# Row-tiled state updates of the samples, and the inverse's second triangle by VectorE's block transposes

## The chip, the core and the metric

One core of a Trainium2 chip. TensorE (PE) multiplies, with its weight loads on a lane of their own (PEld); VectorE (DVE), ScalarE (ACT) and GpSimd (POOL) work on the vectors, SyncE (SP) issues most transfers. The metric is the device time of one launch in microseconds, median of three runs.

## The reference, cut to what matters

Two layers of a hybrid decoder. Each projects 320 tokens (256 of a prompt; 8 samples of 8 tokens) through `W_in`, runs three mixers beside each other (gated DeltaNet, GDN; differential attention; gated linear attention, GLA), projects through `W_out`, and ends in a SwiGLU block. The change touches two pieces. The first is the triangular solve of GDN, whose matrix is the identity plus a strictly lower triangle:

```
A = where(strict, kk * dmat * bh[..., :, None], 0);  M = I + A
sol = triangular_solve(M, [vbeta, kbd], lower=True, unit_diagonal=True)
```

The second is the state update of the samples, in GDN and in GLA, for each head and sample:

```
S_new = S * exp(glast) + einsum('bhck,bhcv->bhkv', kw, u)     # GDN, 128 x 128 a head
S_new = S * exp(blast) + einsum('bchd,bchv->bhdv', kw, vi)    # GLA, 64 x 128 a head
```

The 64 sample tokens lie in 64 rows (partitions), 8 rows a sample.

## The kernel before, in words

**Dense work.** The weights stream in 1,616 units of 128x512. ACT rounds a unit to `whi`, DVE takes the rest as `wlo` (`conv_hi`, `conv_lo`), and PE runs 12 matmuls of 128x320 a unit, in a fixed order. All else on PE (the mixers) is written by tasks (`gdn_prompt`, `gdn_sample`, `gla_prompt`, `gla_sample`, attention) and is put between the dense matmuls by a list scheduler, `Program.order`, which fixes the order of every engine ahead of the launch from its own table of costs. Nearly every instruction is recorded through one helper, so the profile has them all on line 673 and they are told apart by tile and shape. Small matmuls that follow each other and write different quarters of the partitions are kept together as one piece of work by `Program.add` and `_merge`. An fp32 matmul stands once in an order and as two passes in the trace.

**The inverse** (`inverse`, line 1530). It runs on the 32x32 blocks of the diagonal, with R = 128 rows for a prompt chunk (4 blocks, 3 heads, 5 levels) and R = 64 for the samples (2 blocks, 3 heads, 3 levels). A tile `tu` holds the inverse so far (`tu[:,0]`) and its transpose (`tu[:,1]`). Both are kept current by matmuls: first one group against `idb`, then at each level a group that gives `p_`, a copy by ACT, and two groups, one for each form. A group is 12 matmuls of 32x32 for the prompt, 6 for the samples. There are 8 prompt inverses and 4 of samples in the two layers.

**The samples' states.** `gdn_sample` (line 1780) and `gla_sample` (line 2360) hold the states of the 8 samples side by side in a tile `s0` of 128x1024. The update takes two steps `a`, one for each half of the samples: the values are spread over four blocks of 128 columns with the mask `ind8`, a matmul over all 64 rows gives 512 columns, and DVE adds them to half of `s0`. Both steps spread into the same tile, so the second spread waits for the first matmul. In GDN DVE spreads the first and POOL the second; in GLA each step has one spread on either. Then `s0` is written out and the next head's state loaded into it.

**The end of the mixers.** `gate` multiplies GDN's outputs `sv` by the gates, head by head, into `oA` (a rounded copy by ACT, the rest by DVE). The first `out` units of a layer read `oA`.

Of the kernel before, what the change touches and what calls it, by code (L numbers as in the profile page):

```python
# [18 lines left out]
ALU = mybir.AluOpType  # L19
# [274 lines left out]
def raw_ap(x):  # L294
    x = x.ap_ if isinstance(x, LazyAP) else x
    return x if isinstance(x, bass.AP) else x[:]
# [46 lines left out]
class Program:  # L343
# [36 lines left out]
    def add(self, e, name, fn, a, kw, lab, reads, writes):  # L380
        o = Op()
        i = o.i = len(self.ops)
        o.e, o.name, o.fn, o.a, o.kw, o.lab, o.hold = e, name, fn, a, kw, lab, self.hold
        o.func = str(a[2]).split(".")[-1] if name == "activation" else None
        if o.func not in SETS:
            o.func = None
        o.dense = e == "PE" and isinstance(lab, tuple) and lab[0] == "unit" and a[1].dtype == F32R
        out = kw.get("out", a[0] if a else None)
        if e == "PE" and out.shape[0] < 128 and self.ops:
            p = out.start_partition() // 32  # L390
            quads = set(range(p, p + (out.shape[0] + 31) // 32))
            g = self.ops[-1]
            if g.e == "PE" and g.lab == lab and len(g.quads) < 4 and not quads & set(g.quads):
                self._merge(g, o, reads, writes, quads)
                return g
        deps, raw, o.quads, psum = set(), set(), None, False
        for w, aps in ((False, reads), (True, writes)):
            for ap in aps:
                r = region(ap)
                if r is None:  # L400
                    continue
                key, p0, p1, spans = r
                if key.startswith("bank"):
                    psum, spans = True, [(0, 512)]
                    deps.update(self.pre.get(key, ()))
                    self.seen.setdefault(key, []).append(i)
                if w and e == "PE":
                    o.quads = range(p0 // 32, (p1 + 31) // 32)
                    for q in o.quads:
                        if (key, q) in self.chain:  # L410
                            deps.add(self.chain[(key, q)])
                        self.chain[(key, q)] = i
                self._touch(i, key, w, p0, p1, spans, deps, raw)
        if o.dense:
            if self.last_dense is not None:
                deps.add(self.last_dense)
            self.last_dense = i
        deps.discard(i)
        o.preds, o.succs, o.n, o.subs, o.raw, o.table = deps, [], 0, [(fn, a, kw)], raw, None
        self._cost(o, psum)  # L420
        self.ops.append(o)
        return o

    def _merge(self, g, o, reads, writes, quads):

# [295 lines left out]
def emit(nc, pool, psp, T, O, coff, ioff, n_pages):  # L721
# [30 lines left out]
    banks = [psp.tile([128, 512], F32, name=f"bank{i}") for i in range(8)]  # L752
# [32 lines left out]
    def cs(name, rows=slice(0, 128)):  # L785
        a, n = coff[name]
        return cst[rows, a:a + n]


    def mm(out, lhsT, rhs, start=True, stop=True):  # L790
        PE.matmul(out, lhsT, rhs, start=start, stop=stop, skip_group_check=True)
# [6 lines left out]
    def tt(eng, out, a, b, op):  # L798
        eng.tensor_tensor(out=out, in0=a, in1=b, op=op)
# [79 lines left out]
    def ap(h):  # L879
        return h[1][2]  # L880

    def bank(n=1):
        if clk.task.t > clk.t["PE"] + SLACK:
            yield
        while len(dense_free if wide[0] else mix_free) < n:
            yield WAIT
        bs = [(dense_free if wide[0] else mix_free).popleft() for _ in range(n)]
        for b_ in bs:
            prog.epoch(f"bank{b_}")
        return bs if n > 1 else bs[0]  # L890

    def fb(*bs):
        for b in bs:
            free_dense(b)
# [635 lines left out]
    def inverse(aq, k, R, get, keep):  # L1530

        nb = R // 32
        lv = (1, 2, 4, 8, 16) if R == 128 else (1, 2, 4)
        nl = len(lv)
        Ad = yield from get(32 * k)
        ad = ap(Ad)[0:R].rearrange("p (h i) -> p h i", h=k)
        for b in range(nb):
            sl = slice(32 * b, 32 * b + 32)
            (G.tensor_copy if b % 2 else V.tensor_copy)(ad[sl], aq[sl, :, 1, sl])
        LT = yield from get(nl * 32 * k)  # L1540
        lt = ap(LT)[0:R].rearrange("p (s h i) -> p s h i", s=nl, h=k)
        msk = cs("ms", slice(0, R)).rearrange("p (s i) -> p s i", s=5)[:, 0:nl]
        for s in range(nl):
            tt(V, lt[:, s], ad, msk[:, s:s + 1, :].to_broadcast([R, k, 32]), ALU.mult)
        fr(Ad)
        yield
        TU = yield from keep(64 * k)
        tu = ap(TU)[0:R].rearrange("p (t h i) -> p t h i", t=2, h=k)
        idb = cs("idb", slice(0, R))[:, None, :].to_broadcast([R, k, 32])
        bb = yield from bank()  # L1550
        pv_ = banks[bb][0:R, 0:32 * k].rearrange("p (h i) -> p h i", h=k)
        for h in range(k):
            for b in range(nb):
                sl = slice(32 * b, 32 * b + 32)
                mm(pv_[sl, h], lt[sl, 0, h], cs("idb", sl))
        tt(G, tu[:, 1], idb, lt[:, 0], ALU.subtract)
        tt(V, tu[:, 0], idb, pv_, ALU.subtract)
        fb(bb)
        yield
        Ph = yield from get(32 * k)  # L1560
        p_ = ap(Ph)[0:R].rearrange("p (h i) -> p h i", h=k)
        for s in range(1, nl):
            bb = yield from bank()
            pv_ = banks[bb][0:R, 0:32 * k].rearrange("p (h i) -> p h i", h=k)
            for h in range(k):
                for b in range(nb):
                    sl = slice(32 * b, 32 * b + 32)
                    mm(pv_[sl, h], lt[sl, s, h], tu[sl, 0, h])
            A.copy(p_, pv_)
            fb(bb)  # L1570
            yield
            bb = yield from bank()
            pw = banks[bb][0:R, 0:64 * k].rearrange("p (t h i) -> p t h i", t=2, h=k)
            for h in range(k):
                for b in range(nb):
                    sl = slice(32 * b, 32 * b + 32)
                    mm(pw[sl, 0, h], tu[sl, 1, h], p_[sl, h])
                for b in range(nb):
                    sl = slice(32 * b, 32 * b + 32)
                    mm(pw[sl, 1, h], p_[sl, h], tu[sl, 1, h])  # L1580
            tt(V, tu, tu, pw, ALU.subtract)
            fb(bb)
            yield
        fr(LT, Ph)
        return TU
# [194 lines left out]
    def gdn_sample(l, hs):  # L1780
# [9 lines left out]
        TU = yield from inverse(aq, 3, 64, tmp, get)  # L1790
# [7 lines left out]
        for k in range(3):  # L1798
# [34 lines left out]
            stt(osm[:, k], kq[64:128], col["egc"][64:128, 2, h:h + 1], b[64:128, 0:128], ALU.mult, ALU.add)  # L1833
            fb(bb)
            A.activation(sv[:, 9:137], osm[:, k], AF.Square, accum_out=sv[:, k:k + 1])
            for a in range(2):
                wm = ap(E)[0:64].rearrange("p (b v) -> p b v", b=4)
                tt(G if a else V, wm, ws[:, None, :].to_broadcast([64, 4, 128]),
                   cs("ind8", slice(0, 64))[:, 4 * a:4 * a + 4].unsqueeze(2).to_broadcast([64, 4, 128]), ALU.mult)
                yield  # L1840
                bb = yield from bank()
                b = banks[bb]
                mm(b, ap(KW)[0:64], ap(E)[0:64])
                tt(V, ap(S0)[:, 512 * a:512 * a + 512], ap(S0)[:, 512 * a:512 * a + 512], b, ALU.add)
                fb(bb)
            SP.dma_start(O["gs"][l, h], s0)
        fr(WS)
        rms_factor(sv[:, 0:3], sv[:, 3:6], sv[:, 6:9], col["rq"][64:128, 2, h0:h0 + 3])
# [511 lines left out]
    def gla_sample(l, bc, eb):  # L2360
# [29 lines left out]
        for k in range(3):  # L2390
# [18 lines left out]
            tt(V, o[:, k], o[:, k], b2[:, 256:384], ALU.add)  # L2409
            fb(bb[1])  # L2410
            A.activation(st[:, 9:137], o[:, k], AF.Square, accum_out=st[:, k:k + 1])
            for a in range(2):
                for e in range(2):
                    tt(V if e == a else G, four_(w[0:64, 512 * e:512 * e + 512]), vt[:, e:e + 1, :].to_broadcast([64, 4, 128]),
                       cs("ind8", slice(0, 64))[:, 4 * a:4 * a + 4].unsqueeze(2).to_broadcast([64, 4, 128]), ALU.mult)
                bb = yield from bank()
                for e in range(2):
                    h = 2 * k + e
                    mm(banks[bb][64 * e:64 * e + 64, :], kw[:, h * 64:h * 64 + 64], w[0:64, 512 * e:512 * e + 512])
                tt(V, s0[:, 512 * a:512 * a + 512], s0[:, 512 * a:512 * a + 512], banks[bb], ALU.add)  # L2420
                fb(bb)
            SP.dma_start(O["ls"][l, k], s0)
            if k < 2:
                SP.dma_start(s0, T["sgla"][l, k + 1])
# [190 lines left out]
```

## Time and profile before

| | |
|---|---|
| median of 3 runs | 3334.94 us (3334.14 to 3335.1) |
| the profiled execution: its own time, its span | 3333.0 us, 3331.3 us |
| granted TensorE clock, mean | 0.994 |
| PE, PEld, DVE, ACT, POOL busy | 98%, 93%, 59%, 45%, 12% of the span |
| chain that ended last | PE 91%, DVE 3%, DMA 2% |

The mixers of the first layer lie between about 120 and 660 us, those of the second between 1780 and 2320; outside these PE runs dense units nearly alone. PE's busy share counts a matmul from its start to its modelled end, which overlaps its neighbours, so the distance from one start to the next is the better measure.

### The profile page before, as it was taken

To read this page: it belongs to the slowest core of one execution; us is meant where nothing else is said; L and a number is where in the kernel's file an instruction comes from. 1 tells how busy PE (TensorE), PEld (TensorE's weight loads), DVE (VectorE), ACT (ScalarE), POOL (GpSimd) and SP (SyncE) were. 2 spreads that over 40 slices of the span, in tenths; PEclk is the share of its full clock that TensorE was granted. 3 is DMA by queue.
4 is the path that set the end of the run, shared out by engine and by line. 5 is a ranking of instruction groups with operands and counts; after the bars stand their busy time and mean duration, and the time that the engine had idled before them with its cause. 6 is when DMAs were issued, how large, how long until landed. Compare 5 with 4: busy or idle time off the path is not lost.

```text
span 3331.3 us, 69934 instructions
## 1 busy us (share of the span) xinstructions
PE 3271.5 (98%) x26570; PEld 3088.4 (93%) x26570; DVE 1966.5 (59%) x3734; ACT 1491.0 (45%) x3069; POOL 389.1 (12%) x634
## 2 busy tenths in 40 slices
PE   9999999999999999999999999999999999999997
PEld 9987887899999999999999878878999999999997
DVE  5676547886445444544776764588854544454445
ACT  5444444456433443344574543444644334433444
POOL 0234323200000000000002343231000000000000
PEclk9999999999999999999999999999999999999998
DMA  7456654455555555555555577534555555555553
GB/s 227 136 185 213 221 176 122 132 150 156 151 150 149 151 150 149 149 151 150 151 154 142 175 226 225 162 121 148 147 151 149 151 150 150 151 149 149 150 151 114
DMA packets 264404, 527.86 MB, mean 158 GB/s; under 512 B 31362, under 2 KB 33026, under 8 KB 263938
## 3 DMA queue, kind: packets, MB, share of 16 engines
q1 hardware_dynamic: 243586, 456.26, 47.6%
q0 software_dynamic: 20480, 67.13, 6.3%
q8 instruction: 208, 3.41, 0.4%
q14 instruction: 130, 1.06, 0.1%
HBM read 506.25 MB, written 16.36 MB: 157 GB/s over the span
## 4 chain that ended last, share of the span: by engine, by line
PE 91%; DVE 3%; DMA 2%; issue 2%; ACT 1%; POOL 0%; POOLq 0%; SPq 0%; ACTq 0%; DVEq 0%
PE bank L673 91%; DVE gen L673 1%; DVE wlo L673 1%; DMA geng<-in_ck 1%; DMA gen<-in_sgdn 0%; DMA c<-in_sgdn 0%; DVE geng L673 0%; SPq L673 0%; POOLq L2012 0%; DMA out_gs<-gen 0%; POOL geng L673 0%; DMA out_gs<-c 0%; ACT geng L673 0%; DVE blkB L673 0%; DMA raw<-in_win 0%
## 5 line engine op out<-in xcount | busy, mean ns | idle before, releaser
L673 DVE TENSOR_TENSOR wlo<-raw,whi 128x512 fp32r<-128x512 f32 x1616 | 1126.9, 698 | 1110.8 <-PE bank L673 903.3
L673 ACT CAST whi<-raw 128x512 fp32r<-128x512 f32 x1616 | 1002.1, 621 | 1423.9 <-PE bank L673 1347.2
L673 PE MATMUL bank<-xh,wlo 128*128 128x320 f32 (+1 forms) x4544 | 1422.8, 313 | 0.0
L673 PE MATMUL bank<-xh,whi 128*128 128x320 f32 (+1 forms) x4544 | 1416.7, 312 | 4.7 <-ACT xh L673 4.7
L673 PE MATMUL bank<-xl,whi 128*128 128x320 f32 (+1 forms) x4544 | 1416.4, 312 | 0.1
L673 PEld LDWEIGHTS bank<-xh,whi 128*128 128x128 f32 x4544 | 858.2, 189 | 20.8 <-issue 13.4
L673 PEld LDWEIGHTS bank<-xh,wlo 128*128 128x128 f32 x4544 | 859.8, 189 | 8.8 <-issue 5.4
L673 PEld LDWEIGHTS bank<-xl,whi 128*128 128x128 f32 x4544 | 857.6, 189 | 8.8 <-issue 6.2
L673 PE MATMUL bank<-actA,whi 128*128 128x320 f32 x1152 | 255.5, 309 | 0.0
L673 PEld LDWEIGHTS bank<-actA,whi 128*128 128x128 f32 x1152 | 193.0, 188 | 0.4
L673 PE MATMUL bank<-actA,wlo 128*128 128x320 f32 x576 | 178.2, 309 | 0.0
L673 PE MATMUL bank<-actB,whi 128*128 128x320 f32 x768 | 170.5, 309 | 0.0
L673 PE MATMUL bank<-actCh,whi 128*128 128x320 f32 x448 | 138.4, 309 | 0.0
L673 PE MATMUL bank<-actCh,wlo 128*128 128x320 f32 x448 | 138.3, 309 | 0.0
L673 PE MATMUL bank<-actCl,whi 128*128 128x320 f32 x448 | 138.3, 309 | 0.0
L673 PEld LDWEIGHTS bank<-actB,whi 128*128 128x128 f32 x768 | 128.6, 188 | 0.0
L673 PE MATMUL bank<-actB,wlo 128*128 128x320 f32 x384 | 118.6, 309 | 0.0
L673 PE MATMUL bank<-geng,gen 128*32 128x256 f32 (+5 forms) x968 | 111.5, 471 | 6.5 <-DMA geng<-in_ck 4.8
L673 PEld LDWEIGHTS bank<-actA,wlo 128*128 128x128 f32 x576 | 108.3, 188 | 0.1
L673 POOL COPY gen<-g 128x24 f32<-128x24 f32 x18 | 5.8, 328 | 871.9 <-DMA g<-in_scv 870.4
L2014 POOL DMA_DIRECT2D geng<-in_ck x128 | 70.3, 550 | 242.6 <-DVE actA L673 130.9
L673 PEld LDWEIGHTS bank<-g 32*32 32x32 f32 (+2 forms) x2784 | 55.9, 111 | 41.0 <-issue 29.7
(294 smaller groups left out, 3434.7 us busy)
## 6 DMA issues: line engine op xcount, KB each, us to landing
raw<-in_wgu SPq DMA_DIRECT2D x704, 256.0 KB
raw<-in_win SPq DMA_DIRECT2D x434, 256.0 KB
raw<-in_wd SPq DMA_DIRECT2D x352, 256.0 KB
geng<-in_ck POOLq DMA_DIRECT2D x128, 256.0 KB, 3.7
geng<-in_cvp POOLq DMA_DIRECT2D x128, 256.0 KB, 3.8
raw<-in_wout SPq DMA_DIRECT2D x128, 256.0 KB
c<-in_sgdn SPq DMA_DIRECT2D x6, 512.0 KB
out_gs<-c SPq DMA_DIRECT2D x6, 512.0 KB
```

The lines of the kernel that those rows point to most:

```text
L673: fn(*[real(x) for x in a], **{k: real(v) for k, v in kw.items()})
L2014: G.eng.dma_start(out[:, k * 512:k * 512 + 512], src[l, ds(reg, 1)].rearrange(pat))
```

## The change

**Inverse.** The group against `idb` goes: `tu[:,1]` is now taken on DVE (before on POOL) and `tu[:,0]` is its transpose, block by block, by `V.transpose`. At each level only `tu[:,0]` is updated by matmuls; `tu[:,1]` is again DVE's transpose of it. By the orders of the two kernels 552 matmuls of 32x32 go (480 of the prompt, 72 of the samples) and 52 transposes come (40 of 128x96, 12 of 64x96); DVE's subtractions at the levels halve from 192 to 96 columns, and 12 small subtractions move from POOL to DVE.

**State updates.** The values are spread once, with the mask `m4`, which repeats every 32 rows. Rows 0 to 31 hold samples 0 to 3 and rows 32 to 63 samples 4 to 7, so two matmuls over 32 rows each give the two halves, into two banks that are taken together. `_beside` lets the planner keep such matmuls together. The number of matmuls stays (24 in GDN, 24 in GLA); 12 spreads in GDN fall away from POOL, and in GLA 6 each from DVE and POOL.

```diff
+        if e == "PE" and name == "matmul" and self.ops and self._beside(self.ops[-1], o):
+            self._merge(self.ops[-1], o, reads, writes, set(self._cells(a)[1]))
+            return self.ops[-1]
...
+    def _beside(self, g, o):
+
+        if g.e != "PE" or g.name != "matmul" or g.lab != o.lab or o.a[1].shape[0] > 32:
+            return False
+        rows, cols, b = self._cells(o.a)
+        for _, a, _ in g.subs:
+            if a[1].shape != o.a[1].shape:
+                return False
+            r_, c_, b_ = self._cells(a)
+            if set(c_) & set(cols) and (set(r_) & set(rows) or b_ == b):
+                return False
+            if set(r_) & set(rows) and b_ != b:
+                return False
+        return True
...
-        bb = yield from bank()
-        pv_ = banks[bb][0:R, 0:32 * k].rearrange("p (h i) -> p h i", h=k)
-        for h in range(k):
-            for b in range(nb):
-                sl = slice(32 * b, 32 * b + 32)
-                mm(pv_[sl, h], lt[sl, 0, h], cs("idb", sl))
-        tt(G, tu[:, 1], idb, lt[:, 0], ALU.subtract)
-        tt(V, tu[:, 0], idb, pv_, ALU.subtract)
-        fb(bb)
+        tf, tf_ = (ap(TU)[0:R, 32 * k * t:32 * k * t + 32 * k] for t in range(2))
+        tt(V, tu[:, 1], idb, lt[:, 0], ALU.subtract)
+        V.transpose(tf, tf_)
...
             for h in range(k):
                 for b in range(nb):
                     sl = slice(32 * b, 32 * b + 32)
-                    mm(pw[sl, 0, h], tu[sl, 1, h], p_[sl, h])
-                for b in range(nb):
-                    sl = slice(32 * b, 32 * b + 32)
-                    mm(pw[sl, 1, h], p_[sl, h], tu[sl, 1, h])
-            tt(V, tu, tu, pw, ALU.subtract)
+                    mm(pw[sl, h], tu[sl, 1, h], p_[sl, h])
+            tt(V, tu[:, 0], tu[:, 0], pw, ALU.subtract)
             fb(bb)
+            V.transpose(tf_, tf)
...
+            wm = ap(E)[0:64].rearrange("p (b v) -> p b v", b=4)
+            tt(V, wm, ws[:, None, :].to_broadcast([64, 4, 128]),
+               cs("m4", slice(0, 64)).unsqueeze(2).to_broadcast([64, 4, 128]), ALU.mult)
+            yield
+            bb = yield from bank(2)
             for a in range(2):
-                wm = ap(E)[0:64].rearrange("p (b v) -> p b v", b=4)
-                tt(G if a else V, wm, ws[:, None, :].to_broadcast([64, 4, 128]),
-                   cs("ind8", slice(0, 64))[:, 4 * a:4 * a + 4].unsqueeze(2).to_broadcast([64, 4, 128]), ALU.mult)
-                yield
-                bb = yield from bank()
-                b = banks[bb]
-                mm(b, ap(KW)[0:64], ap(E)[0:64])
-                tt(V, ap(S0)[:, 512 * a:512 * a + 512], ap(S0)[:, 512 * a:512 * a + 512], b, ALU.add)
-                fb(bb)
+                sl = slice(32 * a, 32 * a + 32)
+                mm(banks[bb[a]], ap(KW)[sl], ap(E)[sl])
+            for a in range(2):
+                s_ = ap(S0)[:, 512 * a:512 * a + 512]
+                tt(V, s_, s_, banks[bb[a]], ALU.add)
+            fb(*bb)
```

`gla_sample` changes in the same way: two spreads with `m4` ahead of one group of four matmuls (two heads, two halves).

**Three places in the order.** PE, first layer, a level of a prompt's inverse (tile `g`) among attention's small matmuls. Before, a level's two groups are 12 and 24 matmuls:

```order
L673 MATMUL bank_80<-xh,wlo 128x320
L673 MATMUL bank_85<-g_0_90 32x32 x12
L673 MATMUL bank_86<-geng,gen 32x512 x4
L673 MATMUL bank_84<-g_0_90 32x32 x24
L673 MATMUL bank_83<-geng,gen 128x128 x2
```

After, both are 12:

```order
L696 MATMUL bank_81<-xl,whi 128x320
L696 MATMUL bank_85<-g_0_90 32x32 x12
L696 MATMUL bank_84<-geng,gen 32x256 x4
L696 MATMUL bank_82<-blkB,gen 32x64 x4
L696 MATMUL bank_85<-g_0_90 32x32 x12
```

PE, first layer, the first state update of the second three GDN heads (state in tile `gen`). Before, the two halves stand 11 dense matmuls apart:

```order
L673 MATMUL bank_81<-xh,whi 128x320
L673 MATMUL bank_83<-gen 128x512
L673 MATMUL bank_81<-xl,whi 128x320
...
L673 MATMUL bank_81<-xh,wlo 128x320
L673 MATMUL bank_83<-gen 128x512
```

After, they stand side by side:

```order
L696 MATMUL bank_80<-xh,whi 128x320
L696 MATMUL bank_82<-gen 128x512
L696 MATMUL bank_86<-gen 128x512
L696 MATMUL bank_84<-gen 64x128
L696 MATMUL bank_80<-xl,whi 128x320
```

Over the whole program the dense work is interrupted 344 times, before 356 times.

DVE, first layer, the gate of GDN ahead of the first `out` unit (`blkB` holds the gates). Before, the weight conversions `wlo` stand between its parts:

```order
L673 TENSOR_TENSOR blkB<-blkB,sv 128x320 x3
L673 TENSOR_TENSOR wlo<-raw,whi 128x512
L673 TENSOR_TENSOR oA_6448<-blkB,oA_6448 128x320 x3
L673 TENSOR_TENSOR wlo<-raw,whi 128x512
L673 TENSOR_TENSOR oA_6448<-blkB,oA_6448 128x320
```

After, it runs in one piece:

```order
L696 SCALAR_TENSOR_TENSOR blkB<-gen,blkB 128x960 x2
L696 TENSOR_TENSOR blkB<-blkB,sv 128x320 x3
L696 TENSOR_TENSOR oA_6182<-blkB,oA_6182 128x320
L696 TENSOR_TENSOR blkB<-blkB,sv 128x320
L696 TENSOR_TENSOR oA_6182<-blkB,oA_6182 128x320 x5
L696 TENSOR_TENSOR wlo<-raw,whi 128x512 x2
```

On PE the transposes that bring the last three GDN heads of the samples into `sv` stood 85 dense matmuls ahead of the first one that reads `oA`; after the change 25.

## Rows read from the trace of the kernel before

**Rows 1.** The page, busy time of the engines: us, share, instructions.
```profile
PE 3271.5 (98%) x26570; PEld 3088.4 (93%) x26570; DVE 1966.5 (59%) x3734; ACT 1491.0 (45%) x3069; POOL 389.1 (12%) x634
```
**Rows 2.** Stretches: length, busy (x) of PE, PEld, DVE, ACT, POOL, PEclk, DMA share, GB/s.
```profile
440.00:660.00 220.00, 210.32 (x2229) 175.76 (x2228) 162.04 (x306) 98.63 (x225) 67.22 (x60) 0.97 0.43 129
1000.00:1050.00 50.00, 50.00 (x343) 50.00 (x342) 26.10 (x43) 17.57 (x29) 0.00 (x0) 1.00 0.53 152
```
**Rows 3.** Timeline of PE at 448: start, us, engine, line, instruction.
```profile
447.77 0.30 PE L673 MATMUL bank<-xl,whi 128*128 128x320 f32 x1
448.01 0.39 PE L673 MATMUL bank<-g 32*32 32x32 f32 x24
448.33 0.41 PE L673 MATMUL bank<-xh,wlo 128*128 128x320 f32 x1
```
**Rows 4.** Timeline of PE, the dense matmuls around another burst.
```profile
125.80 0.31 PE L673 MATMUL bank<-xl,whi 128*128 128x320 f32 x1
...
126.53 0.42 PE L673 MATMUL bank<-xh,wlo 128*128 128x320 f32 x1
```
**Rows 5.** Groups of PE in 125.7 to 126.9: what that burst holds.
```profile
L673 PE MATMUL bank<-cst,g 32*32 32x32 f32 x24 | 0.4, 192 | 0.0
L673 PE MATMUL bank<-cst,c 32*32 32x32 f32 x12 | 0.4, 194 | 0.0
```
**Rows 6.** Groups of PE by form, whole span: busy us, mean ns | idle before, releasers.
```profile
L673 PE MATMUL bank<-g 32*32 32x32 f32 x2544 | 41.6, 195 | 0.1
...
L673 PE MATMUL bank<-gen,sq 128*32 128x512 f32 x24 | 7.2, 622 | 6.3 <-DMA gen<-in_sgdn 6.3
```
**Rows 7.** Timeline of PE at 167: half a GDN state update alone.
```profile
167.15 0.30 PE L673 MATMUL bank<-xh,whi 128*128 128x320 f32 x1
167.39 1.12 PE L673 MATMUL bank<-c 64*128 64x512 f32 x2
168.44 0.41 PE L673 MATMUL bank<-xl,whi 128*128 128x320 f32 x1
168.69 0.31 PE L673 MATMUL bank<-xh,wlo 128*128 128x320 f32 x1
```
**Rows 8.** Timeline of PE: attention's scores, two row halves, then one.
```profile
347.52 0.70 PE L673 MATMUL bank<-blkB 64*128 64x256 f32 x4
348.15 0.41 PE L673 MATMUL bank<-xh,whi 128*128 128x320 f32 x1
...
355.65 0.70 PE L673 MATMUL bank<-blkB 64*128 64x256 f32 x2
356.27 0.41 PE L673 MATMUL bank<-xl,whi 128*128 128x320 f32 x1
```
**Rows 9.** Timeline of PE: half a GLA state update, two heads, and what follows.
```profile
599.05 1.08 PE L673 MATMUL bank<-geng,gen 64*64 64x512 f32 x4
600.06 0.88 PE L673 MATMUL bank<-geng 128*64 128x128 f32 x12
```
**Rows 10.** Groups of DVE by form, whole span.
```profile
L673 DVE TENSOR_TENSOR g<-g,bank 128x192 f32<-128x192 f32 x32 | 11.3, 352 | 37.3 <-PE bank L673 36.9
L673 DVE TENSOR_TENSOR g<-g,cst 128x96 f32<-128x96 f32 x40 | 8.9, 262 | 1.6 <-POOL g L673 1.6
L673 DVE COPY geng<-geng 32x192 f32<-32x192 f32 x10 | 8.2, 819 | 0.3
```
**Rows 11.** Timeline, the last state updates and the gate of the first layer.
```profile
565.38 1.09 PE L673 MATMUL bank<-gen 64*128 64x512 f32 x2 [1.65 <-ACT geng L673]
...
573.08 0.40 PE L673 MATMUL bank<-cst,gen 64*128 64x64 f32 x3
...
590.75 0.34 PE L673 MATMUL bank<-oA,whi 128*128 128x320 f32 x1
```
**Rows 12.** The same stretch on DVE.
```profile
579.88 4.03 DVE L673 TENSOR_TENSOR blkB<-blkB,sv 128x320 f32<-128x320 f32 x3
...
588.05 0.48 DVE L673 TENSOR_TENSOR oA<-blkB,oA 128x320 fp32r<-128x320 f32 x1
```

More of the change, by code (lines that the diff above doesn't have):

```diff
@@ L422, in add, with _cells @@
         return o
+    def _cells(self, a):
+        k, p = a[1].start_partition() // 32, a[0].start_partition() // 32
+        return (range(k, k + (a[1].shape[0] + 31) // 32), range(p, p + (a[0].shape[0] + 31) // 32), raw_ap(a[0]).name)
+    def _beside(self, g, o):
[11 more added lines that the diff above has]
+        return True
     def _merge(self, g, o, reads, writes, quads):
@@ L1572, in inverse @@
             bb = yield from bank()
-            pw = banks[bb][0:R, 0:64 * k].rearrange("p (t h i) -> p t h i", t=2, h=k)
+            pw = banks[bb][0:R, 0:32 * k].rearrange("p (h i) -> p h i", h=k)
             for h in range(k):
@@ L2411, in gla_sample @@
             A.activation(st[:, 9:137], o[:, k], AF.Square, accum_out=st[:, k:k + 1])
+            for e in range(2):
+                tt(G if e else V, four_(w[0:64, 512 * e:512 * e + 512]), vt[:, e:e + 1, :].to_broadcast([64, 4, 128]),
+                   cs("m4", slice(0, 64)).unsqueeze(2).to_broadcast([64, 4, 128]), ALU.mult)
+            bb = yield from bank(2)
             for a in range(2):
[L2413 to L2416, printed above, removed]
+                sl = slice(32 * a, 32 * a + 32)
                 for e in range(2):
                     h = 2 * k + e
-                    mm(banks[bb][64 * e:64 * e + 64, :], kw[:, h * 64:h * 64 + 64], w[0:64, 512 * e:512 * e + 512])
-                tt(V, s0[:, 512 * a:512 * a + 512], s0[:, 512 * a:512 * a + 512], banks[bb], ALU.add)
-                fb(bb)
+                    mm(banks[bb[a]][64 * e:64 * e + 64, :], kw[sl, h * 64:h * 64 + 64], w[sl, 512 * e:512 * e + 512])
+            for a in range(2):
+                tt(V, s0[:, 512 * a:512 * a + 512], s0[:, 512 * a:512 * a + 512], banks[bb[a]], ALU.add)
+            fb(*bb)
             SP.dma_start(O["ls"][l, k], s0)
```

## The prediction

> **What bounds the kernel now.** I read the page's busy times first. PE is busy for 98% of the span and no other engine for more than 59% [rows 1], so the question is whether that is work or an average that hides waits. [...] In the last part of the first layer's mixers, 440 to 660, PE is still busy for 210 of 220 us at a granted clock of 0.97, with DVE busy for 162 and POOL for 67 [rows 2]. [...] The reader should take from this that a microsecond removed from PE in the mixers is a microsecond off the span, as long as the chains of the mixers still end before the dense work that needs them.
>
> What a mixers' burst costs is read from the timeline, by starts. Around a burst of 24 small passes the dense starts lie 0.56 us apart (447.77 to 448.33) [rows 3]; around one of 36 passes they lie 0.73 apart [rows 4, 5]. Twelve passes more cost 0.17, so 14 ns a pass. Over the whole span 2,544 such passes keep PE busy for 41.6 us, 16.4 ns each [rows 6], which counts the tail of each burst too. Half of a GDN state update takes two passes, and from its start to the next dense one it is 1.05 us (167.39 to 168.44); standing alone it pushes the second dense matmul behind it to 168.69, 1.54 after the one ahead of it. Two dense steps are 0.29 and the passes 1.05, so the interruption itself costs 0.20 [rows 7].
>
> **The change, part by part.** *Inverse, PE.* 552 matmuls go, 1,104 passes. At 15 ns, between the 14 and the 16.4, that is 16.6 us. The upper bound is 1,104 times 16.4, 18.1 us. For the lower one I drop the 144 passes of the samples, whose groups are so small that a burst of them may cost no less when it is halved: 960 times 14 ns is 13.4 us.
>
> *State updates, PE.* If two matmuls over different 32 rows run beside each other, each pair takes what one takes now. Twelve second halves in GDN at 1.05 us are 12.6 us. In GLA one half with its two heads takes 1.01 us from its start to the next group (599.05 to 600.06) [rows 9]; six of them are 6.1 us. Does the chip run two row halves side by side? Attention shows it by chance. Once its two score matmuls, which read the upper and the lower 64 rows and write different banks, stand together: four passes from 347.52 to the next dense start at 348.15, 0.63 us. Alone, two passes take from 355.65 to 356.27, 0.62 us [rows 8]. The second pair is free. Thirty-two rows in place of 64 are not shown here, so the bounds are nothing and the whole 18.7; I take the whole, since the nearest row shows no loss at all.
>
> *Interruptions.* Twelve fewer, at 0.20, are 2.4 us. If all twelve bursts fell away only in part, this is nothing.
>
> PE's sum is 16.6 + 12.6 + 6.1 + 2.4 = 37.7 us.
>
> *DVE.* Fifty-two transposes are new, and no row shows one. The nearest row, 96 columns from memory to memory, takes 0.262 us; the dearest plain copy of similar size takes 0.819 [rows 10]. I take 0.26, 13.6 us in all, and keep 0.82 (42.6 us) for the range. Against it the 36 subtractions of a level shrink from 192 columns (0.352 us) towards 96 (about 0.26), 3.3 us less, and 12 small ones come from POOL, 3.1 us more. So DVE gains some 13 us over two layers. I cost that at nothing: in the busiest stretch DVE has 58 of 220 us free [rows 2], and a transpose is not what comes next in its chain. The next level's first group reads `tu[:,0]`, which the subtraction has just written; only the second group reads the transpose, after PE's first group and ACT's copy. Behind a transpose in DVE's queue stand the weight conversions, and PE waits for these if DVE falls behind by the lead of its buffers. Without cover the price is the full 13.6. [...]
>
> *Chains.* A head's update had two steps in a row, which read and wrote one spread tile. In the second three heads of GDN they now become one, so `s0` is written out, and the next head's load behind it on SP's queue issues, that much earlier. PE also eats the dense units faster, though. What is late next is the gate. Before, the samples' last outputs were transposed at 573.08 and the first `out` matmul started at 590.75, 17.7 us later [rows 11]; DVE's last part of `oA` ended at 588.53 [rows 12]. After the change only 24 dense matmuls stand between, and the whole gate is one piece on DVE. Behind the transposes (0.40) come three products (4.03 together [rows 12]), one more and six subtractions at 0.48 each: about 7.8 us. PE reaches the sixth block of `oA` after 24 and 15 dense matmuls, 5.7 us. It waits some 2 us a layer, 4 in all. The lower bound is nothing, if the products find their inputs early. The upper one is the chain as long as it was: 588.53 less 573.08 is 15.5, less 5.7, so 9.8 a layer and 19.6 in all.
>
> **The sum.** 3331.3 - 37.7 + 4 = 3297.6 us of span. The profiled execution's own time was 1.7 above its span, and the runs' median is 1.9 above that execution: 3301 us.
>
> **The rivals.** *The row tiles take turns.* Then the 18.7 us of the state updates stay, PE saves 37.7 - 18.7 - 4 = 15 and the time is 3320. Attention's pair speaks against it [rows 8], though its tiles have 64 rows; for it speaks only that no row shows 32. [...]
>
> *The gate comes too late.* PE's savings ahead of `oA` are about 31 us in two layers (all but GLA's), so PE arrives some 15 us earlier a layer. If the sample chain moves less than that, because its loads and DVE's queue set it and not PE, the wait is nearer its upper bound, 15 to 20 us in all: 3313 to 3317. For it speaks how short the lead has become in the order; against it that the chain loses a whole step a head.
>
> *Waits of before close as well.* The trace has PE waiting 1.65 us for ACT ahead of one state update [rows 11] and 6.3 us for the second heads' states [rows 6]. If the shorter chains take these, a wait of the first kind in either layer and most of the second kind, 8 us, and the gate costs nothing, the time is 3289.
>
> *DVE becomes the bound.* This ends on the other side. If a transpose takes 0.82 us and none of it is covered, the conversions behind it make PE wait 42.6 us and the time is 3344. It decides from 33.7 / 52 = 0.65 us uncovered a transpose. The 58 us free in the busiest stretch speak against it.
>
> *The change does not do what it says:* PE's work shrinks and the time stays, since the stream of weights sets the pace of the mixers. The DMA share is 0.43 in 440 to 660 and 0.53 in the dense stretch [rows 2], so there is room, and I give this little: 3335.
>
> **How the numbers follow.** Forecast as summed, within 3294 to 3309: 0.56. Gate late: 0.16. Row tiles in turn: 0.08. Waits close too: 0.12. DVE the bound: 0.04. No effect: 0.04. The range takes in the forecast, the waits closing up to 3286, and the late gate and the turns up to 3320; with tails it leaves out somewhat less than 2 in 10. A difference of 0.2%, 6.7 us, is what a measurement of this kernel can tell from none. The first four cases end faster by more than that save for a tail, 0.89; no effect and some of the tails are the same, 0.06; DVE's case is slower, 0.05.
>
> **What would show it.** In the changed kernel's profile: the two passes of each half of a state update start some 0.01 us apart and not 1.05, and a GDN update ends 1.05 us after its start; the level's second burst holds 24 passes, and dense starts around it lie 0.56 apart; transposes take 0.2 to 0.3 us, with no more waits of PE for `wlo` than before; PE waits a few microseconds at the first `oA` matmuls of each layer. A wait of 8 us or more there, passes of the halves that follow each other, or transposes over 0.65 us would make the prediction wrong.

## The result, and the profile after

The changed kernel takes 3295.5 us (median of 4 runs, 3293.1 to 3298.7), the kernel before, run beside it, 3335.0: a ratio of 0.988, with a 95% interval of 0.986 to 0.990. The time fell by 39.5 us; 33.9 was forecast. Run again beside 17 executions of the kernel before (e5), the changed kernel took 3295.8 us and that one 3330.5, which is 34.7 less: the changed kernel's time repeats, and the 3335.0 of four executions was high for the kernel before. The profiled execution took 3294.5 us, its span is 3292.7. The sum is off by less than 6 us, but the experiments show that two of its terms were off by more, one upwards and one downwards. That these errors cancelled so well is in part luck.

The page's busy line answers to [rows 1]:

```profile
PE 3235.2 (98%) x25466; PEld 3072.3 (93%) x25466; DVE 1959.6 (60%) x3780; ACT 1493.2 (45%) x3069; POOL 359.7 (11%) x604
```

PE is still busy for 98% of the span: it has less work, not more room. DVE has 7 us less in the sum, though it took on 52 transposes; the prediction had it gain some 13. Three stretches (columns as in [rows 2]):

```profile
440.00:660.00 220.00, 208.11 (x2152) 179.56 (x2152) 170.59 (x337) 102.97 (x231) 60.68 (x54) 0.98 0.46 139
563.40:566.80 3.40, 3.40 (x14) 3.40 (x15) 3.40 (x8) 2.23 (x6) 1.94 (x1) 0.56 0.09 12
1000.00:1050.00 50.00, 50.00 (x343) 50.00 (x342) 26.11 (x43) 17.55 (x29) 0.00 (x0) 1.00 0.54 152
```

The dense stretch is as it was: 343 matmuls touch 50 us, 0.146 us from start to start, at a granted clock of 1.00, as in [rows 2]. DVE now works 171 of the 220 us of the busiest stretch, where it had 162. The row in the middle lies just behind a wait of PE at the gate; "what was not expected" returns to it.

The timeline of PE, by starts, in six places: the bursts of 24 and of 12 passes (with the dense matmul ahead of them and the second one behind), a GDN update and what follows it, the first `oA` matmul of layer 0, a GLA update, the first `oA` matmul of layer 1:

```profile
149.26 0.31 PE L696 MATMUL bank<-xh,wlo 128*128 128x320 f32 x1
149.50 0.39 PE L696 MATMUL bank<-g 32*32 32x32 f32 x24
150.07 0.31 PE L696 MATMUL bank<-xl,whi 128*128 128x320 f32 x1
...
162.53 0.30 PE L696 MATMUL bank<-xl,whi 128*128 128x320 f32 x1
162.76 0.38 PE L696 MATMUL bank<-g 32*32 32x32 f32 x12
163.32 0.31 PE L696 MATMUL bank<-xh,whi 128*128 128x320 f32 x1
...
167.27 0.31 PE L696 MATMUL bank<-xh,whi 128*128 128x320 f32 x1
167.50 1.13 PE L696 MATMUL bank<-c 32*128 32x512 f32 x4
168.56 0.38 PE L696 MATMUL bank<-g 32*32 32x32 f32 x18
...
562.63 0.41 PE L696 MATMUL bank<-oA,whi 128*128 128x320 f32 x1 [2.48 <-ACT oA L696]
...
625.81 1.09 PE L696 MATMUL bank<-geng,gen 32*64 32x512 f32 x8
626.83 0.42 PE L696 MATMUL bank<-oA,whi 128*128 128x320 f32 x1
...
2193.25 0.41 PE L696 MATMUL bank<-oA,whi 128*128 128x320 f32 x1 [2.31 <-ACT oA L696]
```

A whole GDN update is now four passes that take 1.06 us from their start to the next group (167.50 to 168.56); half of one took 1.05 in [rows 7]. A GLA update with both halves and both heads takes 1.02 (625.81 to 626.83), where half of one took 1.01 in [rows 9]. The timeline merges the four passes; one by one, those of the update at 167.50 start 0, 0.007, 0.534 and 0.540 us after its start, so the two halves stand 0.007 us apart. The row tiles do run side by side. (The prediction's sign speaks of the two passes of each half; it means the halves, as the passes of one half lie 0.53 apart.) At `oA` PE waits 2.48 and 2.31 us.

Groups of PE by form, answering to [rows 6]:

```profile
L696 PE MATMUL bank<-g 32*32 32x32 f32 x1776 | 31.2, 194 | 0.0
L696 PE MATMUL bank<-geng,gen 32*64 32x512 f32 x48 | 6.6, 619 | 1.5 <-DVE geng L696 1.5
L696 PE MATMUL bank<-gen 32*128 32x512 f32 x24 | 6.8, 640 | 0.0
L696 PE MATMUL bank<-c 32*128 32x512 f32 x24 | 6.8, 640 | 0.0
L696 PE MATMUL bank<-gen,sq 128*32 128x512 f32 x24 | 6.4, 601 | 3.5 <-DMA gen<-in_sgdn 3.4
```

2,544 passes have become 1,776 here; the rest of the 1,104 is in groups of other names. The updates keep PE busy for 20.2 us (6.6 + 6.8 + 6.8) where the three groups of before took 14.0, 13.5 and 13.4. The waits for the next head's state in `gen` are 3.4 us, 6.3 before. Groups of DVE by form, answering to [rows 10]:

```profile
L696 DVE TENSOR_TENSOR g<-g,bank 128x96 f32<-128x96 f32 x32 | 8.0, 249 | 13.8 <-PE bank L696 13.8
L696 DVE STREAM_TRANSPOSE g<-g 128x96 f32<-128x96 f32 x40 | 10.9, 271 | 0.8
L696 DVE STREAM_TRANSPOSE gen<-gen 64x96 f32<-64x96 f32 x6 | 1.6, 268 | 0.1
L696 DVE STREAM_TRANSPOSE blkC<-blkC 64x96 f32<-64x96 f32 x6 | 1.6, 264 | 0.0
```

A transpose of 128x96 takes 0.271 us, one of 64x96 some 0.266; 0.26 had been assumed from a plain row. A level's subtraction fell from 0.352 to 0.249 us. No run here has a transpose of another width, so what part of the 0.271 us goes by the columns is left open.

### The profile page after: what moved, and what is told of

Its sections match the earlier page's. It is cut to its first block, busy times and chain, and to the rows that moved or that the text cites. A ratio compares the mean times of both kernels' runs of the same rounds, so it can differ in the third digit from the quotient of the medians.

```text
span 3292.7 us, 67703 instructions
## 1 busy us (share of the span) xinstructions
PE 3235.2 (98%) x25466; PEld 3072.3 (93%) x25466; DVE 1959.6 (60%) x3780; ACT 1493.2 (45%) x3069; POOL 359.7 (11%) x604
## 3 DMA queue, kind: packets, MB, share of 16 engines
q14 instruction: 128, 1.05, 0.1%
## 4 chain that ended last, share of the span: by engine, by line
PE 76%; issue 2%; DVE 1%; DMA 1%; ACT 0%; POOL 0%; POOLq 0%; SPq 0%; ACTq 0%; DVEq 0%
PE bank L696 76%; DVE gen L696 0%; POOLq L2029 0%; DMA geng<-in_ck 0%; DVE wlo L696 0%; DVE geng L696 0%; POOL geng L2031 0%; DVE blkB L696 0%; DMA out_gs<-gen 0%; DMA gen<-in_sgdn 0%; DMA c<-in_sgdn 0%; ACT blkB L696 0%; DVE c L696 0%; POOL blkB L696 0%; ACT accq L696 0%
## 5 line engine op out<-in xcount | busy, mean ns | idle before, releaser
L696 PE MATMUL bank<-geng,gen 128*32 128x256 f32 (+5 forms) x968 | 101.8, 466 | 7.3 <-DMA geng<-in_ck 4.4
L696 PE MATMUL bank<-oA,whi 128*128 128x320 f32 x384 | 92.7, 325 | 5.3 <-ACT oA L696 4.8
```

Source lines behind the costliest of these rows:

```text
L696: fn(*[real(x) for x in a], **{k: real(v) for k, v in kw.items()})
```

## The experiments

All times are medians of several runs, and each is to be read beside the kernel before as it ran on the same chip (3330.7 us for the first four, 3330.5 for the next four, 3332.1 for the last). The executions of one kernel spread over 5 to 15 us, and a difference of two medians is good to some 2 to 4 us either way. Kernels e1 to e4 and e12 change the program, so the planner lays out the order of all engines anew. In e6 to e11 the planner works with the old entries and only what is issued in each place differs, so that PE's dense and mixers' matmuls stand in the same order as in the parent kernel (an interruption whose only work is dropped goes).

For the traces I keep an account that no single view has. I take the steps from each PE start to the next and put each to one of these: steps from one mixers' matmul to another; steps into and out of the mixers' stretches; PE's waits over 0.25 us that another engine or a DMA ended (without the one at the start of the kernel); and the other steps that begin while the granted clock is lowered ("in half clock": from 563.40 to 566.00 of the changed kernel it is 0.50). (Steps between dense matmuls at full clock are the rest: 2823 us before and after.) An interruption is a stretch of mixers' matmuls between two dense ones.

| profiled execution | interruptions | among mixers' | in and out | waits | in half clock | span |
|---|---|---|---|---|---|---|
| before | 356 | 311.2 | 120.0 | 30.3 | 19.4 | 3331.3 |
| changed | 344 | 288.4 | 109.6 | 28.3 | 16.6 | 3292.7 |
| e5 changed, again | 344 | 288.1 | 109.9 | 33.5 | 13.0 | 3294.9 |
| e1 inverse only | 384 | 285.6 | 133.8 | 38.6 | 29.0 | 3333.6 |
| e2 states only | 359 | 302.7 | 114.6 | 32.0 | 16.4 | 3316.5 |
| e6 inverse, old order | 354 | 299.4 | 122.3 | 35.5 | 27.3 | 3332.6 |
| e9 no reload | 356 | 310.8 | 119.7 | 23.7 | 17.2 | 3322.0 |
| e10 no reload, inverse | 354 | 302.0 | 122.9 | 27.0 | 13.0 | 3316.6 |
| e7 same rows, held | 344 | 300.1 | 108.4 | 28.8 | 23.6 | 3309.4 |
| e8 passes back, held | 344 | 294.9 | 110.1 | 30.7 | 13.7 | 3300.3 |

The second and third rows are two executions of one program. The two columns of the mixers' steps repeat (398.0 us together in both), but the waits differ by 5.2 us and the half clock by 3.6, so smaller differences in these two columns show nothing.

**e1, the inverse alone.** The changed kernel with the samples' updates of before.

```diff
             for a in range(2):
-                sl = slice(32 * a, 32 * a + 32)
-                mm(banks[bb[a]], ap(KW)[sl], ap(E)[sl])
...
+                mm(b, ap(KW)[0:64], ap(E)[0:64])
```

> The new inverse alone; the state updates are those of before. Theory (PE's passes and interruptions add up): 1,104 passes at 15 ns are 16.6 us less, but the planner's order interrupts the dense work 384 times, 28 times more than before, which at 0.20 us is 5.6 us more: 3324 us, give or take 5. Rival (only the passes count, interruptions are free): 3318 us. Second rival (the passes are hidden and the whole gain is the states' shorter chain): 3335 us.

Measured: 3336.3 us, 1.002 of before (1.001 to 1.003). With the order that the planner gave it, the inverse alone gains nothing; it loses 5.7 us. In the account the time among mixers' matmuls fell by 25.6 us, but 28 more interruptions brought 13.8 us of steps in and out, PE waits 8.3 us more, and 9.6 us more are spent at half clock. PE's waits (us in total, times, longest; the same three are 5.4, 6.3 and 4.8 in before):

```profile
PE bank L696 <- DVE gen L696: 10.2, 12, 1.4
PE bank L696 <- DMA gen<-in_sgdn: 7.2, 4, 3.4
PE bank L696 <- DMA geng<-in_ck: 7.1, 6, 1.8
```

**e2, the states alone.** The changed kernel with the inverse of before.

```diff
+                for b in range(nb):
+                    sl = slice(32 * b, 32 * b + 32)
+                    mm(pw[sl, 1, h], p_[sl, h], tu[sl, 1, h])
...
+            tt(V, tu, tu, pw, ALU.subtract)
...
-            V.transpose(tf_, tf)
```

> The new state updates alone; the inverse is that of before. Theory: 12 halves of GDN at 1.05 us and 6 of GLA at 1.01 us are 18.7 us less, interruptions 359 against 356, so 3317 us, give or take 5. Rival (the shorter chain of a head, and not PE's passes, is what gains): nearly all of the 39.5 us comes with this part, 3298 us. Second rival (the row tiles take turns): 3335 us.

Measured: 3321.9 us, 0.997 (0.996 to 0.998), 8.8 us below before, at the upper edge of the expected time. The two halves together (5.7 lost, 8.8 won) do not give the 35 to 40 us of the whole. The account says where to look: against before, the whole change has 12 interruptions fewer, while e1 has 28 and e2 has 3 more; the waits are 8.3 us more in e1 (those of the change and of e2 differ from before by no more than two executions of one program do). This points to the planner's order, which is laid out anew for each program.

**e3, same rows.** Both halves of an update read rows 0 to 31, so that they should no longer run beside each other (in e7, with the same rows, a GDN update takes 1.91 us, 1.06 in the changed kernel).

```diff
-                sl = slice(32 * a, 32 * a + 32)
+                sl = slice(0, 32)
```

> The changed kernel, but both halves of a state update read rows 0 to 31, so that they can't run beside each other; the second half of the states gets wrong values, all else stays. Theory (the overlap of the two row tiles is the gain): 18.7 us more for the passes and 16 interruptions more (360 against 344) at 0.20, so 22 us over the changed kernel, 3317 us. Rival (the gain is the chain that lost a step, with one spread and both matmuls together): the chain is as short as in the changed kernel, so 3296 to 3300 us. In the trace the theory wants the starts of the two halves about 1.05 us apart.

Measured: 3316.8 us, 0.996 (0.994 to 0.997). As the overlap wants it, but with 16 more interruptions than the changed kernel, so e7 repeats it with the order held.

**e4, the passes put back.** The 432 matmuls of the levels are issued again, into columns that nobody reads.

```diff
+            px = banks[bb][0:R, 32 * k:64 * k].rearrange("p (h i) -> p h i", h=k)
...
+                    mm(px[sl, h], p_[sl, h], tu[sl, 1, h])
```

> The changed kernel with the second group of each level's second step computed again, into columns that nobody reads; the transposes stay. 432 matmuls, 864 passes come back. Theory: at 14 to 15 ns a pass 12 to 13 us more, with 3 interruptions fewer about 12 us, so 3307 us. Rival (what the inverse gains is a shorter chain, the passes run beside other work): 3296 us.

Measured: 3324.8 us, 0.998 (0.997 to 0.999), 29 us above the changed kernel and more than twice the expected. Its profiled execution waits 41.9 us and has 48.2 us at half clock, the changed kernel's 28.3 and 16.6. Its steps of the mixers outside the half clock are 401.3 us, only 3.3 above the changed kernel's. So most of it came with waits and half clock, in a new order, and not with the passes; this execution was also among the slowest of its twelve. e8 repeats it with the order held.

**e5, the changed kernel again,** unchanged, so that the next three have it beside them.

> The changed kernel itself, so that the three beside it have it on their own chip: 39.5 us below the kernel before, as the first time, within 3 us.

Measured: 3295.8 us (3292.4 to 3299.4), 0.989 (0.988 to 0.990). That is 34.7 us below the kernel before, not 39.5 within 3: the expectation was missed, through the kernel before, which ran at 3330.5 here.

**e6, the new inverse in the order of before.** What the planner records stays; what is issued in its place is swapped.

```diff
+            for fn, a, kw in self.swap.get(o.i, o.subs):
...
                     mm(pw[sl, 1, h], p_[sl, h], tu[sl, 1, h])
+                prog.swap[prog.ops[-1].i] = []
             tt(V, tu, tu, pw, ALU.subtract)
+            prog.swap[prog.ops[-1].i] = [(nc.vector.tensor_tensor, (), dict(out=tu[:, 0], in0=tu[:, 0], in1=pw[:, 0], op=ALU.subtract)),
+                                 (nc.vector.transpose, (tf_, tf), {})]
```

> The kernel before with the changed inverse, but the planner is not told: it sets the order with the costs of before, and only what is issued in each place differs (552 small matmuls fall away, 52 transposes come to VectorE). Theory that the price of 15 ns a pass was right and that the planner's new order took it back in the run with the inverse alone: 16.6 us below the kernel before, 14 to 18. Rival, the passes are not on the path that sets the end and PE waits instead: within 3 us of the kernel before. Rival, the transposes on VectorE make PE wait: at or above the kernel before.

Measured: 3326.3 us, 0.9987 (0.9978 to 0.9995): 4.2 us below before (1.7 to 7.3), not 14 to 18. So the planner's order is not the whole story of e1, and in this order the passes do not bring 15 ns each. The profiled execution was the slowest of its twelve (3334.2); in it PE waits 5.2 us more than in before, and 7.9 us more are in half clock. One such wait, first as it was in before, and the clock in two stretches around it:

```profile
181.03 0.62 PE L673 MATMUL bank<-c,sq 128*32 128x512 f32 x1 [0.70 <-DMA c<-in_sgdn]
```

```profile
182.25 1.06 PE L674 MATMUL bank<-c,sq 128*32 128x512 f32 x1 [2.56 <-DMA c<-in_sgdn]
```

```profile
172.00:182.00 10.00, 7.70 (x58) 7.11 (x57) 6.51 (x12) 3.74 (x8) 1.71 (x2) 1.00 0.63 199
182.00:186.00 4.00, 3.75 (x18) 2.08 (x19) 1.71 (x2) 0.59 (x1) 1.70 (x1) 0.58 0.41 156
```

PE waits 2.56 us for the load of the next head's state, 0.70 in before. It is there 0.64 us earlier (179.69 against 180.33), and the wait ends 1.22 us later; why it ends later is not shown. From 182 to 186 the granted clock is 0.58.

**e7, same rows, order held.** The edit in GLA is the same.

```diff
                 mm(banks[bb[a]], ap(KW)[sl], ap(E)[sl])
+                g = prog.ops[-1]
+                g.subs[-1] = (g.subs[-1][0], (banks[bb[a]], ap(KW)[0:32], ap(E)[0:32]), g.subs[-1][2])
```

> The changed kernel in its own order, but both halves of a state update read the same 32 rows, so that they cannot run side by side (the second half of each state gets wrong values). Theory of overlapping row tiles: 18.7 us above the changed kernel, 16 to 20. Rival, the first run of this kind got its 21 us from the planner's new order and not from the rows: within 5 us of the changed kernel.

Measured: 3310.8 us, 0.994 (0.992 to 0.995), 15.0 us above e5. The same GDN update and the same GLA update as shown of the changed kernel:

```profile
168.09 1.98 PE L696 MATMUL bank<-c 32*128 32x512 f32 x4
170.00 0.38 PE L696 MATMUL bank<-g 32*32 32x32 f32 x18
...
632.08 1.93 PE L696 MATMUL bank<-geng,gen 32*64 32x512 f32 x8
633.95 0.41 PE L696 MATMUL bank<-oA,whi 128*128 128x320 f32 x1
```

They take 1.91 and 1.87 us, not 1.06 and 1.02. The second half costs 0.85 us when it cannot overlap, and 18 of them are 15.3 us: the rows and the time of the whole agree. (The forecast 18.7 is within 4 us of the time as well; it is the rows that decide for 15.3.) One by one, the passes of the update at 168.09 start at 0, 0.532, 0.962 and 1.391 us, and no longer in pairs. In the account the mixers' steps rise by 10.5 us only, as one of the 18 updates fell into half clock and took 3.7 us there.

**e8, the passes put back, order held.** As e4, but appended behind the planner.

```diff
+                g = prog.ops[-1]
+                for b in range(nb):
+                    sl = slice(32 * b, 32 * b + 32)
+                    g.subs.append((g.subs[0][0], (px[sl, h], p_[sl, h], tu[sl, 1, h]), g.subs[0][2]))
```

> The changed kernel in its own order, with the 864 passes of the inverse's levels issued again in the same bursts, into columns of the bank that nobody reads. Theory of 15 ns a pass: 13 us above the changed kernel, 11 to 15. Rival, such passes cost 30 ns and more, as the run with the planner told seemed to say: 26 us or more above it.

Measured: 3307.2 us, 0.993 (0.992 to 0.994), 11.4 us above e5, within the expected 11 to 15: 13 ns a pass. In the account it is less: 7.0 us more among, in and out than e5 (405.0 against 398.0), 8 ns a pass. The profiled execution was the fastest of its six (3302.1), and the median is good to 4 us, so the two figures meet at their edges. The burst of 24 passes shown above has 48 here:

```profile
150.43 0.31 PE L696 MATMUL bank<-xh,wlo 128*128 128x320 f32 x1
150.66 0.62 PE L696 MATMUL bank<-g 32*32 32x32 f32 x48
151.47 0.31 PE L696 MATMUL bank<-xl,whi 128*128 128x320 f32 x1
```

From the dense matmul ahead to the second one behind it is 1.04 us with 48 passes, 0.81 with 24 (149.26 to 150.07) and 0.79 with 12 (162.53 to 163.32). Less two dense steps of 0.146, a burst costs 0.75, 0.52 and 0.50 us. All bursts of such passes alone, at full clock, say the same: in the changed kernel 0.50 for 12 passes (four bursts), 0.51 to 0.52 for 24 (18 bursts) and 0.69 to 0.70 for 36 (eight); in e8 0.74 to 0.75 for 48 (16) and 1.12 for 72 (four).

**e9 and e10, without reloads.** Is it the load of the next state that eats the inverse's gain in the old order? e9 is the kernel before, in its order, without the loads of the later states; e10 adds the inverse of e6.

```diff
             SP.dma_start(s0, T["sgdn"][l, h])
+            if k:
+                prog.swap[prog.ops[-1].i] = []
...
                 SP.dma_start(s0, T["sgla"][l, k + 1])
+                prog.swap[prog.ops[-1].i] = []
```

> The kernel before in its own order, without the loads of the second and later states of a mixer (20 of 24 loads of sample states in two layers are in question, of 1 MB in all ways together half a megabyte each; the later heads then start from the earlier head's state, so their results are wrong). It is the base for the next run. PE waited 8.6 us for GDN's states in the trace of before; what of it falls away is at most that: 0 to 8 us below the kernel before.

> The same without the loads, but with the changed inverse in the order of before. In the run with the loads the inverse saved only some 4 us where its passes are worth 12 to 16. Theory that PE, arriving earlier, waits longer for the next state's load: without the loads the inverse saves 10 us or more against the run beside it. Rival, what eats the gain is the chain of VectorE and the half-clock stretches behind any wait: again some 4 us against the run beside it, within 3.

The first of these counts wrongly: 12 of 18 loads fall away, 8 of GDN's 12 and 4 of GLA's 6. Measured: e9 3323.1 us, 0.997 (0.996 to 0.998); e10 3318.4 us, 0.996 (0.995 to 0.998). The loads are worth 9.1 us, a little more than the 0 to 8 expected, and the inverse gains 4.7 us on e9, as little as with them. So the loads are not the cause, and that theory falls. The rival has the number right, but what it names does not show: the half clock of e10 is 4.2 us below that of e9. In the account the time among, in and out falls by 5.6 us between e9 and e10, 5 ns a pass, and the waits rise by 3.3.

If the mixers' steps in half clock are counted as well, at half their length, the three pairs with a held order come together: 8.2 us from before to e6, 7.6 from e9 to e10, 7.3 from e5 to e8, which is 7.4, 6.9 and 8.4 ns a pass. So on average, with all the bursts that they lie in, the passes are worth about half of the 15 ns.

**e11, each transpose three times,** order held.

```diff
             V.transpose(tf_, tf)
+            prog.ops[-1].subs *= 3
```

> The changed kernel in its own order, each of the 52 transposes issued three times in a row: 104 more of 0.27 us, 28 us more of VectorE. Theory that transposes are hidden at nothing: within 3 us of the changed kernel (3295). Rival, they stand in the mixers' chains or hold up the weight conversions: 28 us above it. Half covered: some 14.

Measured: 3296.5 us, 0.990 (0.988 to 0.991): 35.6 us below the kernel before beside it, where e5 was 34.7 below. DVE's largest group alone shows 22.3 of the 28 us more of work; none of it can be seen in the time:

```profile
L696 DVE STREAM_TRANSPOSE g<-g 128x96 f32<-128x96 f32 x120 | 33.2, 276 | 3.5
```

**e12, the gate's products on DVE.** In the changed kernel the long product on POOL ends at 561.11, and ACT's first roundings begin right behind it. POOL's second product, behind the long one, ends at 562.09; ACT's third rounding begins behind that, and it is the one that ends PE's wait at 562.63. First POOL, then ACT, by timeline:

```profile
558.26 2.85 POOL L696 TENSOR_TENSOR blkB<-blkB,sv 128x320 f32<-128x320 f32 x1 [3.09 <-ACT whi L696]
...
561.23 0.86 POOL L696 TENSOR_TENSOR blkB<-blkB,sv 128x320 f32<-128x320 f32 x1
```

```profile
561.14 0.82 ACT L696 CAST oA<-blkB 128x320 fp32r<-128x320 f32 x2 [0.82 <-POOL blkB L696]
562.12 1.54 ACT L696 CAST oA<-blkB 128x320 fp32r<-128x320 f32 x4 [0.15 <-POOL blkB L696]
```

```diff
-                tt(G if h == h0 else V, z[:, h], z[:, h], o[:, h, :], ALU.mult)
+                tt(V, z[:, h], z[:, h], o[:, h, :], ALU.mult)
```

> The changed kernel with all six products of the GDN gate on VectorE; two of the six were GpSimd's, whose 2.85 us product ended just before the wait of PE at the first output matmul (2.48 and 2.31 us). Theory that this product sets the wait: some 1.5 us less a layer, 2 to 4 us below the changed kernel in all. Rival, the planner's order or VectorE takes it back: within 2 us of the changed kernel.

Measured: 3295.7 us, 0.989 (0.987 to 0.990): 36.4 us below the kernel before beside it, the same as e5 within the spread. PE's waits for ACT at `oA` did fall by half:

```profile
562.57 0.41 PE L696 MATMUL bank<-oA,whi 128*128 128x320 f32 x1 [1.27 <-ACT oA L696]
...
2194.47 0.94 PE L696 MATMUL bank<-oA,whi 128*128 128x320 f32 x2 [1.27 <-ACT oA L696]
```

But PE starts there at the same time as in the changed kernel (562.57 against 562.63): it came 1.15 us later, and the gate was ready no earlier. Its waits for DVE, counted as in the account, are 20.3 us over the span (14.4 and 16.3 in the two executions of the changed kernel). A wait was moved, not removed. No run beats the changed kernel clear of the spread.

## Why the prediction was right, by its steps

**PE's work is paid in full: right on the whole, and only there.** 98% busy before and after, and the time fell with the work. With the order held, e7 and e8 give back 15.0 and 11.4 of the 34.7 us, by the overlap of the row tiles and by 864 of the 1,104 passes. But the planner's order, waits and half-clock stretches move the time by 10 us and more from program to program (e1 against e6, e4 against e8), as much as the terms of the sum.

**State updates, 18.7 us: the mechanism right, the size too large.** The overlap is there, and e7 takes it away at 15.0 us. The term took half an update at 1.05 us from its first start to the next dense one; that contains 0.20 us of the entry into the burst, which stays. By e7's rows the second half itself is 0.85 us, and 18 of those are 15.3.

**Inverse, 16.6 us, not below 13.4: this step failed.** In the order of before it is worth 4.2 us (e6) and 4.7 (e10). In the order of the changed kernel 864 of the 1,104 passes are worth 11.4 (e8), which taken alone is near the forecast price. By the account, which does not hang on waits, a pass costs 5 to 9 ns in all three pairs, or 7 to 8 with the steps in half clock counted at half length. That is about 8 us for the 1,104, half of the term. What takes 3 to 4 us more from it in e6 and e10 is within the spread of the medians and stays open.

The 14 ns came from one pair of bursts, 24 and 36 passes [rows 3 to 5]. The pair was read rightly and is typical of its two sizes, but the line through it does not go on: 12 passes cost as much as 24 (0.50 and 0.52 us), 36 cost 0.69, 48 only 0.75, and 72 again 1.12, so that no one price a pass fits them. Most of the change at the levels is from 48 passes to 24, which buys 0.23 us, 10 ns a pass. The lower bound left out the samples' small groups because a burst may have a floor, but it kept the prompt's passes at the full 14 ns, those inside large mixed bursts too. What makes this floor no run here shows.

**Interruptions, 2.4 us: too small.** Twelve fewer were read rightly from the order (356 to 344), but at 0.20 us each. A burst of 12 or 24 passes costs 0.50, and an update's half alone 1.25 [rows 7], of which the passes are 0.85 and the entry 0.40. So the 0.20 us by which a half was priced too high is the 0.20 by which an interruption was priced too low; for a half that stood alone the two cancel. The steps in and out fell by 10.4 us in all. This and the planner's regrouping made up for the inverse: by the account the mixers' steps fell by 33.2 us, of which the states are 15 (by e7) and the inverse some 6 to 10; the remaining 8 to 12 come with the order. How much of it is the twelve interruptions (5 to 6 at 0.40 to 0.50) and how much regrouping was not separated.

**DVE, nothing: right.** Transposes take 0.271 us, no wait of PE for `wlo` shows before or after (its weight loads, PEld, wait 3.7 us for it before and 7.6 after), and e11 shows that even three times as many are covered (3296.5 us, 3295.8 in e5). This rival is out. The sum of DVE's work was wrong: some 13 us more were expected, and the page shows 6.9 less. The six spreads of GLA that leave DVE (0.94 us each in before) had not been taken off; the rest was not followed up.

**The gate, 4 us: right in size and place, not in cause.** PE waits 2.48 and 2.31 us at the first `oA` matmul. The price came from DVE's chain, which was to hold PE up at the sixth block, with 4.03 us for three products [rows 12]. After the change DVE's three products take 1.27 us, PE waits only 0.25 us for DVE at `oA` in each layer, and what ends last is ACT's rounding behind POOL's two products, which had no term. So that the size came out is in part luck. e12 shows that the wait is no gain to be had by itself.

**The gate comes too late** did not come about: 4.8 us of waits in all, not 15 to 20.

**Waits of before close as well: not seen in the sum.** PE no longer waits 1.65 us for ACT ahead of the late update [rows 11], and the wait for states in `gen` went from 6.3 to 3.4 (3.9 in e5). New waits took it back: the sum without the start of the kernel is 30.3 us before, and 28.3 and 33.5 in the two executions of the changed kernel.

**The row tiles take turns** is refuted by the rows of the updates and by e7. **No effect** is refuted for the whole, but e1 came out as that rival put it for the inverse.

So the number came out by a sum of three terms, of which one was a few us too high, one about twice too high and one several times too low. The whole change was forecast within 6 us; its parts alone were missed by 12 (e1) and by 5 (e2). The overlap of the row tiles was understood; that the sum came so near was luck as well.

## What to carry to other kernels

Price small work on PE by the interruption first and by the pass second, from bursts of at least three sizes, and look for a floor: halving a burst that lies on it bought next to nothing here (24 passes cost 0.52 us, 12 cost 0.50), and joining two bursts buys the entry of one, by the estimate from [rows 7] and e7 0.40 us. Where a planner lays out the order, its number of interruptions and its waits are terms of their own, and parts of a change need not add up (5.7 us lost in e1 and 8.8 won in e2, 39.5 won by the whole); test a part in an order that is held still, and read a run with a new order as a test of both. A wait that is shortened at one place gives nothing if PE waits the longer ahead of it in the same chain: in e12 the wait at `oA` fell from 2.48 to 1.27 us, and the time stayed (3295.7 us, 3295.8 in e5).

## What was not expected of the hardware

The floor of a burst: 12 and 24 passes of 32x32 hold the dense matmuls up by 0.50 and 0.52 us, 36 by 0.69 and 48 by 0.75.

The granted clock fell to 0.50 behind some short waits. In the changed kernel PE waits 2.48 us before 562.63, and from 563.40 to 566.80 the granted clock is 0.56 on average, 0.50 up to 566.00: 14 dense matmuls touch 3.4 us, and 343 touch 50 at full clock. Of the 3.4 us some 1.4 are lost (14 at 0.146 are 2.0). So the wait of 2.48 us came with a loss of some 1.4 more. Every trace in the table of the account has steps in half clock (13.0 to 29.0 us); there are 5 such stretches in the changed kernel ahead of the end and 6 in the kernel before. The five of the changed kernel stand behind waits of 1.51 to 2.48 us; behind its wait of 1.51 us at 538.6, and behind the shorter ones of the mixers, it did not fall. The spread of one kernel's executions goes with the granted clock: of the 17 of the kernel before beside e5, the fastest (3325.1 us) had a mean of 0.996 and the slowest (3338.1) 0.992. That the stretches make this spread is likely, but was not shown.
